# One-hot tiles of the column keys, written by VectorE token by token instead of number by number

## The chip, the core and the metric

The kernel runs on one core of one Trainium2 chip. The metric is the device time of one execution in microseconds (us), the median of three runs. The core's engines are called as in the profile: PE is TensorE's matmuls, PEld its weight loads, DVE VectorE, ACT ScalarE, POOL GpSimd, SP SyncE, whose queue issues the plain DMAs.

## What is computed

One inference step of a two-layer decoder for 512 prompt tokens and 8 sample tokens. Layer 0 is a gated MLP, layer 1 differential attention, and a PEER block stands behind each. PEER picks, for every token and each of 8 heads, 16 of 16,384 experts by two small top-16 searches (a row key and a column key, 128 each), and adds the chosen experts' outputs. The part of the reference that matters here:

```python
s = jnp.einsum('thcd,hcnd->thcn', q, keys)
sv, si = lax.top_k(s, PEER_TOPK)
...
cidx = si[:, :, 0, :, None] * N_KEYS + si[:, :, 1, None, :]
top_s, pos = lax.top_k(cand, PEER_TOPK)
eidx = jnp.take_along_axis(cidx, pos, axis=-1)
g = jax.nn.softmax(top_s, axis=-1)
act = jax.nn.gelu(jnp.einsum('thkd,td->thk', u_tab[eidx], h))
return jnp.einsum('thk,thkd->td', (g * act).astype(h.dtype), v_tab[eidx])
```

## The kernel before

PEER is done in two ways at once. For two of the four prompt tiles of 128 tokens in each layer (256 tokens), `dense_peer` goes through all 16,384 experts with matmuls. For the other two, `peer_tile` gathers the chosen rows by indirect DMA, 256 rows of u and of v (128x1024 each) per tile, and DVE multiplies them (lines 715 and 722). These 512 gathers a layer are spread over the dense work: a table of anchors ties each of them to an instruction of the dense part, and the scheduler that writes each engine's order of instructions keeps them behind it. Every engine then runs its instructions in the fixed order of the built program.

The dense part goes through the experts in four quarters `q` of 32 row keys each (`QI` = 32, with 128 column keys to a row key).

- `acts(q)` (lines 478 to 500): for each row key, the 128 experts' activations for 256 tokens, with u from DMA. In quarter 0 these are fp32 matmuls (line 494). In the others u is split into a high and a low part by ACT (`wh`, line 209) and DVE (`wl`, line 211), and three series of 8 matmuls follow (lines 488, 489, 491). The gelu goes into `W`.
- `gates(q)` (lines 502 to 537): the gate of each token and expert, as a product of two one-hot matrices. For each token there is a stationary operand `ohj` (128 picked experts x 128 column keys, f16: 1 where the expert has that column key) and a moving operand `gi` (128 picked experts x 32 row keys, the gate where the row key fits). Two matmuls (line 533; the gate's high and low half) give a token's 128x32 gates, each with its own weight load of `ohj`. `W` is multiplied by the result (line 536).
- `y` (lines 565 to 576): the gated activations times v, summed over all experts in PSUM.

A tile of `ohj` holds 8 tokens, 1,024 numbers per partition. In each group of four tiles (32 tokens) the first `J_DVE[layer][q]` are written by DVE and the others by ACT. With `J_DVE = [[2, 1, 1, 1], [2, 2, 2, 2]]` and 8 groups to a quarter, DVE writes 40 tiles in layer 0 and 64 in layer 1, which is 104 of 256.

- DVE (line 520): one instruction compares the column keys of 8 tokens with `iotaJ` (128x8 numbers, each column key eight times). The tile is stored number by number: key 0 for all 8 tokens, key 1 for all 8 tokens, and so on. The 128 weights of one token then stand 8 elements (16 bytes) apart.
- ACT (lines 526 and 529): eight instructions |iota - key|, one for each token, and one relu(1 - x) over the tile. The tile is stored token by token: the 128 weights of one token are adjacent.

The weight load of line 533 reads `oh[:, :, k]`, strided from the first kind of tile and packed from the second.

The gates of quarter 0 run beside `acts(1)` before the first `y`. The gates of the later quarters run beside `y` of the quarter before them:

```python
        for _ in gates(0):
            for _ in range(2):
                next(na, None)
```

Of the kernel before, what the change touches and what calls it, by code (L numbers as in the profile page):

```python
# [11 lines left out]
HF = mybir.dt.float16  # L12
# [23 lines left out]
def body(ctx: ExitStack, tc: tile.TileContext, a):  # L36
# [26 lines left out]
    rows = [128, 128, 128, 128, NB]  # L63
    iota128 = const("iota128", [128, 128])

    iotaJ = per.tile([128, 128, 8], HF, name="iotaJ")
    V.tensor_copy(iotaJ, iota128[:, :, None].to_broadcast([128, 128, 8]))
    msk64 = const("msk64", [64, H, 16])
    r64 = const("r64", [64, NB])
    r64f = per.tile([64, NB], FR, name="r64f")  # L70
# [328 lines left out]
    def topk_pick(p, nh, state, layer, gp, out):  # L399
        sv, si, ts, pos = [v[:p] for v in state]  # L400
        n = nh * 16
        tmp = wk.tile([128, 1024], F32, name="tmp", tag="tmp", bufs=1)[:p]
        t1, t2 = [tmp[:, k * 128:k * 128 + n].bitcast(U32) for k in range(2)]
        af, st = [tmp[:, k * 128:k * 128 + n] for k in (2, 3)]
        ab = tmp[:, 512:640].bitcast(HF).rearrange("p (c n) -> p c n", c=2)[:, :, :n]
        sib = tmp[:, 640:768].bitcast(HF)[:, :2 * n].rearrange("p (c k h) -> p c k h", c=2, k=16)
        ij = tmp[:, 768:1024].rearrange("p (c n) -> p c n", c=2)[:, :, :n]
        V.tensor_copy(sib.rearrange("p c k h -> p h c k"), si)

        g = ts if gp is None else gp.tile([128, nh, 16], F32, name="gate", tag="gate", bufs=2)[:p]  # L410
        sm = small(p, nh, "gs")
        V.tensor_copy(sm[:, :, None], ts[:, :, 0:1])
        V.tensor_tensor(g, ts, sm[:, :, None].to_broadcast([p, nh, 16]), op=OP.subtract)
        SC.activation(g, g, AF.Exp)
        yield

        pf = pos.rearrange("p h k -> p (h k)")
        V.tensor_scalar(t1, pf, 4, None, op0=OP.logical_shift_right)
        V.tensor_scalar(t2, pf, 2, None, op0=OP.logical_shift_right)
        V.scalar_tensor_tensor(af, t2, -12.0, t1, op0=OP.add, op1=OP.max)  # L420
        V.scalar_tensor_tensor(af, pf, -72.0, af, op0=OP.add, op1=OP.max)
        yield
        V.tensor_scalar(st, af, 4.0, 48.0, op0=OP.mult, op1=OP.add)
        V.scalar_tensor_tensor(st, af, 16.0, st, op0=OP.mult, op1=OP.min)
        V.scalar_tensor_tensor(st, af, 72.0, st, op0=OP.add, op1=OP.min)

        kh = [ab[:, c].rearrange("p (k h) -> p h k", k=16) for c in range(2)]
        V.tensor_copy(kh[0], af.rearrange("p (h k) -> p h k", h=nh))
        V.tensor_tensor(kh[1], pos, st.rearrange("p (h k) -> p h k", h=nh), op=OP.subtract)
        yield  # L430
        V.tensor_reduce(sm, g, axis=AX.X, op=OP.add)
        V.reciprocal(sm, sm)
        V.tensor_tensor(g, g, sm[:, :, None].to_broadcast([p, nh, 16]), op=OP.mult)
        yield
        for c in range(2):
            oh = wk.tile([128, 16, n], HF, name="oh", tag="junk", bufs=1)[:p]
            m, w = n // 8, 8
            V.tensor_tensor(oh.rearrange("p x (m w) -> p x m w", m=m),
                            ab[:, c, None, :].rearrange("p x (m w) -> p x m w", m=m).to_broadcast([p, 16, m, w]),
                            iotaJ[:p, :16, None, :w].to_broadcast([p, 16, m, w]), op=OP.is_equal)  # L440
            yield
            o4 = oh.rearrange("p x (k h) -> p x k h", k=16)
            V.tensor_tensor(o4, o4, sib[:, c, :, None, :].to_broadcast([p, 16, 16, nh]), op=OP.mult)
            yield
            for x in (8, 4, 2):
                V.tensor_tensor(oh[:, :x], oh[:, :x], oh[:, x:2 * x], op=OP.add)
            V.tensor_tensor(ij[:, c, :].rearrange("p (h k) -> p k h", h=nh),
                            oh[:, 0].rearrange("p (k h) -> p k h", k=16),
                            oh[:, 1].rearrange("p (k h) -> p k h", k=16), op=OP.add)
            yield  # L450
        V.tensor_scalar(ij[:, 1], ij[:, 1], float(layer * NE), None, op0=OP.add)
        out += [ij, g, tmp]
# [16 lines left out]
    def dense_peer(layer, dpa, open_rest, open_odd, smp):  # L469
# [32 lines left out]
        def gates(q):  # L502
# [4 lines left out]
            for t0 in range(0, 256, 32):  # L507

                gi = dpb.tile([128, 2, 16, QI, 2], HF, name="gi", tag="gi", bufs=2)
                sv = [z[:, t0:t0 + 32].rearrange("p (m w) -> p m w", w=2)[:, :, None, :].to_broadcast([128, 16, QI, 2])  # L510
                      for z in (sq, selb[:, 2], selb[:, 3])]
                V.tensor_tensor(gi[:, 1], sv[0], iotaP[:, None, :QI, :].to_broadcast([128, 16, QI, 2]), op=OP.is_equal)
                for k in range(2):
                    V.tensor_tensor(gi[:, k], gi[:, 1], sv[1 + k], op=OP.mult)  # L514
                for t1 in range(t0, t0 + 32, 16):
                    ps = pt.tile([128, QI, 16], F32, name="ps_g", tag="tr")
                    for t2 in range(t1, t1 + 16, 8):
                        oh = dpb.tile([128, 128, 8], HF, name="ohj", tag="ohj", bufs=4)
                        if (t2 // 8) % 4 < J_DVE[layer][q]:
                            V.tensor_tensor(oh, selb[:, 1, None, t2:t2 + 8].to_broadcast([128, 128, 8]), iotaJ,  # L520
                                            op=OP.is_equal)
                        else:

                            oh = oh.rearrange("p j k -> p (j k)").rearrange("p (k j) -> p j k", k=8)
                            for k in range(8):
                                SC.activation(oh[:, :, k], iota128, AF.Abs, scale=-1.0,  # L526
                                              bias=selJ[:, t2 + k:t2 + k + 1])
                            oh2 = oh.rearrange("p j k -> p k j")
                            SC.activation(oh2, oh2, AF.Relu, bias=1.0, scale=-1.0)
                        for k in range(8):  # L530
                            t = t2 + k
                            for c in range(2):
                                PE.matmul(ps[:, :, t - t1], oh[:, :, k], gi[:, c, (t - t0) // 2, :, t % 2], start=c == 0,  # L533
                                          stop=c == 1)
                    wv = W[q][:, :, t1:t1 + 16]
                    tick(V.tensor_tensor(wv, ps, wv, op=OP.mult), [[4, 7, 3, 3], [3, 1, 1, 1]][layer][q])
                    yield
# [3 lines left out]
        drain()  # L541
        dpb, py = open_rest()

        iotaP = dpb.tile([128, 128, 2], HF, name="iotaP")
        V.tensor_copy(iotaP, iotaJ[:, :, :2])
        y = [[py.tile([128, 512], F32, name=f"y{t}{hf}", tag=f"y{t}{hf}") for hf in range(2)] for t in range(2)]
        odd = open_odd()
        na = acts(1)
# [657 lines left out]
```

## Time and profile before

| | us |
|---|---|
| median of 3 runs (lowest, highest) | 3229.25 (3229.22, 3231.66) |
| the profiled execution | 3223.32 |
| its span in the trace | 3221.6 |
| PE busy | 2987.1 (93%) |
| DVE busy | 2435.9 (76%) |
| ACT busy | 1306.8 (41%) |
| POOL busy | 1339.0 (42%) |

The span runs from the first to the last instruction of the program; the profiled execution takes 1.7 us more than it. Busy times are of whole engines over the whole span. Matmuls overlap, so their busy time is a union of modelled durations; in a timeline, a row with xN is N instructions that follow each other, with the time from the first's start to the last's end.

### The profile page before, as it was taken

To read this page: it belongs to the slowest core of one execution; us is meant where nothing else is said; L and a number is where in the kernel's file an instruction comes from. 1 tells how busy PE (TensorE), PEld (TensorE's weight loads), DVE (VectorE), ACT (ScalarE), POOL (GpSimd) and SP (SyncE) were. 2 spreads that over 40 slices of the span, in tenths; PEclk is the share of its full clock that TensorE was granted. 3 is DMA by queue.
4 is the path that set the end of the run, shared out by engine and by line. 5 is a ranking of instruction groups with operands and counts; after the bars stand their busy time and mean duration, and the time that the engine had idled before them with its cause. 6 is when DMAs were issued, how large, how long until landed. Compare 5 with 4: busy or idle time off the path is not lost.

```text
span 3221.6 us, 49841 instructions
## 1 busy us (share of the span) xinstructions
PE 2987.1 (93%) x18048; PEld 2237.7 (69%) x18048; DVE 2435.9 (76%) x5119; ACT 1306.8 (41%) x2940; POOL 1339.0 (42%) x1061
## 2 busy tenths in 40 slices
PE   7998979999999999999789988788799999999999
PEld 7898646788558758767687643455689658758767
DVE  1389779769877687789646788879979886686785
ACT  2344021246564573655343333321246443363444
POOL 0035672014554354455511665534234454344340
PEclk9999989999999999999999988799899999999999
DMA  7678987458999899999976989867778999889895
GB/s 246 227 278 303 332 330 247 157 194 305 376 375 366 304 353 357 338 355 368 353 245 203 368 317 320 279 245 269 273 263 305 351 356 360 326 315 357 321 318 171
DMA packets 271561, 976.53 MB, mean 303 GB/s; under 512 B 30938, under 2 KB 31770, under 8 KB 271306
## 3 DMA queue, kind: packets, MB, share of 16 engines
q0 software_dynamic: 152064, 553.72, 47.4%
q1 hardware_dynamic: 119250, 419.62, 36.5%
q8 instruction: 142, 2.33, 0.3%
q14 instruction: 105, 0.86, 0.1%
HBM read 966.76 MB, written 6.46 MB: 302 GB/s over the span
## 4 chain that ended last, share of the span: by engine, by line
PE 66%; DVE 11%; DMA 11%; issue 6%; ACT 4%; POOL 3%; SPq 0%; DVEq 0%; POOLq 0%; ACTq 0%
PE y L576 18%; PE ps_d L231 8%; PE ps_a L494 6%; PE ps_a L488 6%; PE ps_a L489 6%; PE ps_a L491 5%; PE ps_g L533 5%; DMA gath<-peer_v,ix 4%; DMA gath<-peer_u,ix 3%; POOL gath L706 3%; DVE x L722 2%; ACT ohj L526 2%; DVE gath L715 2%; DVE si L369 1%; DMA page<-cache_v 1%
## 5 line engine op out<-in xcount | busy, mean ns | idle before, releaser
L706 POOL DMA_INDIRECT gath<-peer_u,ix x512 | 652.3, 1274 | 921.9 <-DVE gath L715 316.7
L706 POOL DMA_INDIRECT gath<-peer_v,ix x512 | 649.1, 1268 | 700.2 <-DVE x L722 350.9
L722 DVE SCALAR_TENSOR_TENSOR x<-gath,act,x 128x1024 f32<-128x1024 f32 x512 | 655.4, 1280 | 66.0 <-DMA gath<-peer_v,ix 59.5
L576 PE MATMUL y<-vb,W 128*128 128x512 f32 x1536 | 697.8, 600 | 2.1 <-DMA vb<-peer_v 2.1
L715 DVE SCALAR_TENSOR_TENSOR gath<-gath,h_g 128x1024 f32<-128x1024 f32 x512 | 614.8, 1218 | 97.4 <-DMA gath<-peer_u,ix 96.2
L576 PEld LDWEIGHTS y<-vb,W 128*128 128x128 f32 x1536 | 280.7, 191 | 297.0 <-issue 294.3
L231 PE MATMUL ps_d<-hT,wt 128*128 128x128 f32 (+3 forms) x2048 | 432.6, 370 | 28.8 <-DMA wt<-peer_wq 6.7
L526 ACT ACTIVATE ohj<-iota,selJ 128x128 f16<-128x128 f32 x1216 | 367.1, 387 | 216.3 <-PE ps_g L533 215.8
L488 PE MATMUL ps_a<-hPh,wh 128*128 128x256 f32 x1536 | 400.8, 298 | 14.7 <-ACT wh L209 14.7
L231 PEld LDWEIGHTS ps_d<-hT,wt 128*128 128x128 f32 x2048 | 306.3, 200 | 141.5 <-issue 21.0
L489 PE MATMUL ps_a<-hPl,wh 128*128 128x256 f32 x1536 | 384.3, 287 | 0.0
L211 DVE TENSOR_TENSOR wl<-ub,wh 128x1024 fp32r<-128x1024 f32 x192 | 234.6, 1223 | 196.7 <-ACT wh L209 179.2
L488 PEld LDWEIGHTS ps_a<-hPh,wh 128*128 128x128 f32 x1536 | 298.4, 194 | 29.5 <-ACT wh L209 17.2
L209 ACT ACTIVATE wh<-ub 128x1024 fp32r<-128x1024 f32 x192 | 202.0, 1054 | 274.6 <-PE ps_a L489 246.0
L489 PEld LDWEIGHTS ps_a<-hPl,wh 128*128 128x128 f32 x1536 | 298.4, 194 | 10.8 <-issue 10.8
L494 PE MATMUL ps_a<-hT,ub 128*128 128x256 f32 x1024 | 229.6, 386 | 25.1 <-ACT W L499 25.1
L494 PEld LDWEIGHTS ps_a<-hT,ub 128*128 128x128 f32 x1024 | 197.0, 194 | 54.4 <-ACT W L499 25.9
L533 PEld LDWEIGHTS <-ohj 128*128 128x128 f16 x4096 | 190.8, 127 | 62.5 <-issue 48.4
L499 ACT ACTIVATE W<-ps_a 128x256 f32<-128x256 f32 x256 | 95.6, 379 | 341.7 <-PE ps_a L491 180.8
L491 PE MATMUL ps_a<-hPh,wl 128*128 128x256 f32 x1536 | 223.1, 288 | 1.9 <-DVE wl L211 1.9
L533 PE MATMUL ps_g<-gi,ohj 128*128 128x32 f16 x4096 | 197.0, 206 | 12.4 <-DVE gi L514 9.4
L491 PEld LDWEIGHTS ps_a<-hPh,wl 128*128 128x128 f32 x1536 | 200.2, 193 | 9.0 <-issue 5.8
(299 smaller groups left out, 3810.4 us busy)
## 6 DMA issues: line engine op xcount, KB each, us to landing
ub<-peer_ut SPq DMA_DIRECT2D x256, 512.0 KB, 5.8
vb<-peer_v SPq DMA_DIRECT2D x256, 512.0 KB, 6.5
wt<-w_in SPq DMA_DIRECT2D x64, 512.0 KB, 4.5
wt<-peer_wq SPq DMA_DIRECT2D x64, 512.0 KB, 4.7
wt<-w_out SPq DMA_DIRECT2D x32, 512.0 KB, 5.4
gath<-peer_u,ix POOLq DMA_INDIRECT x512, 6.7
gath<-peer_v,ix POOLq DMA_INDIRECT x512, 6.9
wt<-w_k SPq DMA_DIRECT2D x16, 512.0 KB, 5.6
```

Source lines behind the costliest of these rows:

```text
L211: tick(V.tensor_tensor(wl, w, wh.bitcast(F32), op=OP.subtract), k)
L231: z = PE.matmul(ps[:, :n], wt[:, c, :], rhs[:, c0 + c, :n], start=c0 + c == 0, stop=c0 + c == nk - 1)
L488: PE.matmul(ps, uh[:, c, :], hP[0][:, c, :], start=c == 0, stop=False)
L489: PE.matmul(ps, uh[:, c, :], hP[1][:, c, :], start=False, stop=False)
L491: PE.matmul(ps, ul[:, c, :], hP[0][:, c, :], start=False, stop=c == 7)
L494: z = PE.matmul(ps, u[:, c, :], hT[:, c, :256], start=c == 0, stop=c == 7)
L526: SC.activation(oh[:, :, k], iota128, AF.Abs, scale=-1.0, bias=selJ[:, t2 + k:t2 + k + 1])
L533: PE.matmul(ps[:, :, t - t1], oh[:, :, k], gi[:, c, (t - t0) // 2, :, t % 2], start=c == 0, stop=c == 1)
L576: PE.matmul(y[t][hf], w[:, ts], v[:, hs], start=i == 0, stop=i == 127)
L706: GP.indirect_dma_start(out=t, out_offset=None, in_=table, in_offset=bass.IndirectOffsetOnAxis(ap=ix[:, k:k + 1], axis=0))
L715: z = V.scalar_tensor_tensor(u, u, 1.0, h, op0=OP.mult, op1=OP.mult, accum_out=act[:, k:k + 1])
L722: z = V.scalar_tensor_tensor(x[t], v, act[:, k:k + 1], x[t], op0=OP.mult, op1=OP.add)
```

## The change

DVE's tiles are stored token by token as well. For that, the column keys are written twice each into a new tile `selJ2` (256 tokens x 2), and the comparison of line 520 goes over 8 tokens x 64 pairs of keys x 2, so that its innermost run is two adjacent numbers. `iotaJ` (1,024 numbers) is replaced by `iotaH` (128), for that comparison, and `iota8` (16x8), for the top-16 searches; `iotaP` shrinks from 256 numbers to 64. All weight loads of the gates now read a packed `oh[:, k, :]`. ACT's instructions and the numbers that are computed stay the same.

```diff
-    iotaJ = per.tile([128, 128, 8], HF, name="iotaJ")
-    V.tensor_copy(iotaJ, iota128[:, :, None].to_broadcast([128, 128, 8]))
+    iotaH = per.tile([128, 128], HF, name="iotaH")
+    V.tensor_copy(iotaH, iota128)
+    iota8 = per.tile([128, 16, 8], HF, name="iota8")
+    V.tensor_copy(iota8, iota128[:, :16, None].to_broadcast([128, 16, 8]))
...
-                        oh = dpb.tile([128, 128, 8], HF, name="ohj", tag="ohj", bufs=4)
+
+                        oh = dpb.tile([128, 8, 128], HF, name="ohj", tag="ohj", bufs=4)
                         if (t2 // 8) % 4 < J_DVE[layer][q]:
-                            V.tensor_tensor(oh, selb[:, 1, None, t2:t2 + 8].to_broadcast([128, 128, 8]), iotaJ,
-                                            op=OP.is_equal)
+                            V.tensor_tensor(oh.rearrange("p k (m w) -> p k m w", w=2),
+                                            selJ2[:, t2:t2 + 8, None, :].to_broadcast([128, 8, 64, 2]),
+                                            iotaH[:, None, :].to_broadcast([128, 8, 128])
+                                            .rearrange("p k (m w) -> p k m w", w=2), op=OP.is_equal)
                         else:
-
-                            oh = oh.rearrange("p j k -> p (j k)").rearrange("p (k j) -> p j k", k=8)
                             for k in range(8):
-                                SC.activation(oh[:, :, k], iota128, AF.Abs, scale=-1.0,
+                                SC.activation(oh[:, k, :], iota128, AF.Abs, scale=-1.0,
                                               bias=selJ[:, t2 + k:t2 + k + 1])
...
-                                PE.matmul(ps[:, :, t - t1], oh[:, :, k], gi[:, c, (t - t0) // 2, :, t % 2], start=c == 0,
+                                PE.matmul(ps[:, :, t - t1], oh[:, k, :], gi[:, c, (t - t0) // 2, :, t % 2], start=c == 0,
...
-        iotaP = dpb.tile([128, 128, 2], HF, name="iotaP")
-        V.tensor_copy(iotaP, iotaJ[:, :, :2])
+        iotaP = dpb.tile([128, QI, 2], HF, name="iotaP")
+        V.tensor_copy(iotaP, iotaH[:, :QI, None].to_broadcast([128, QI, 2]))
+        selJ2 = dpb.tile([128, 256, 2], HF, name="selJ2")
+        V.tensor_copy(selJ2, dd["sel"][1][:, 1, :, None].to_broadcast([128, 256, 2]))
```

The scheduler writes the orders anew, so some instructions move. On DVE, where the gates of layer 0's quarter 0 begin, the order before is:

```order
L545 COPY iotaP<-iotaJ 128x256
L506 TENSOR_SCALAR selq<-selb 128x256
L520 TENSOR_TENSOR ohj<-selb,iotaJ 128x1024 x2
L512 TENSOR_TENSOR gi<-selq,iotaP 128x1024 x2
L514 TENSOR_TENSOR gi<-gi,selb 128x1024 x4
```

At the same place on DVE, the order of the changed kernel (whose line numbers are 2 to 4 higher) is:

```order
L547 COPY iotaP<-iotaH 128x64
L549 COPY selJ_4455<-selb 128x512
L508 TENSOR_SCALAR selq<-selb 128x256
L523 TENSOR_TENSOR ohj<-selJ_4455,iotaH 128x1024 x2
L514 TENSOR_TENSOR gi<-selq,iotaP 128x1024 x2
L516 TENSOR_TENSOR gi<-gi,selb 128x1024 x4
```

One copy (`selJ2`, printed as `selJ_4455`) has come in ahead of the first two `ohj` and of the `gi` behind them; the rest stands as it stood.

A little later in the same quarter, where the `wl` of `acts(1)` alternate with the gathered tiles (`x_70<-gath` is line 722, `gath,act<-gath` line 715), DVE's order before is:

```order
L512 TENSOR_TENSOR gi<-selq,iotaP 128x1024
L722 SCALAR_TENSOR_TENSOR x_70<-gath,act,x_70 128x1024
L514 TENSOR_TENSOR gi<-gi,selb 128x1024
L722 SCALAR_TENSOR_TENSOR x_70<-gath,act,x_70 128x1024
L514 TENSOR_TENSOR gi<-gi,selb 128x1024
L722 SCALAR_TENSOR_TENSOR x_70<-gath,act,x_70 128x1024
L211 TENSOR_TENSOR wl<-ub,wh 128x1024
L520 TENSOR_TENSOR ohj<-selb,iotaJ 128x1024
L536 TENSOR_TENSOR W<-ps_g,W 128x32x16
```

At that place DVE's order in the changed kernel is:

```order
L514 TENSOR_TENSOR gi<-selq,iotaP 128x1024
L726 SCALAR_TENSOR_TENSOR x_70<-gath,act,x_70 128x1024
L516 TENSOR_TENSOR gi<-gi,selb 128x1024
L726 SCALAR_TENSOR_TENSOR x_70<-gath,act,x_70 128x1024
L516 TENSOR_TENSOR gi<-gi,selb 128x1024
L213 TENSOR_TENSOR wl<-ub,wh 128x1024
L726 SCALAR_TENSOR_TENSOR x_70<-gath,act,x_70 128x1024
L523 TENSOR_TENSOR ohj<-selJ_4455,iotaH 128x1024
L538 TENSOR_TENSOR W<-ps_g,W 128x32x16
```

A `wl` has changed places with one gathered tile. Moves of this kind, mostly by a few places, occur all through the dense part of both layers, on every engine, and here and there in layer 1's attention, where the rest of the gathers is placed. Each engine still has the same work between the start and the end of each part, up to one or two gathered tiles.

## Rows read from the trace of the kernel before

**Rows 1.** The page: busy time by engine, and the chain that ended last.

```profile
PE 2987.1 (93%) x18048; PEld 2237.7 (69%) x18048; DVE 2435.9 (76%) x5119; ACT 1306.8 (41%) x2940; POOL 1339.0 (42%) x1061
...
PE 66%; DVE 11%; DMA 11%; issue 6%; ACT 4%; POOL 3%; SPq 0%; DVEq 0%; POOLq 0%; ACTq 0%
```

**Rows 2.** Tile view of `ohj`: ns min/median/max, first and last start, form.

```profile
L533 PEld LDWEIGHTS <-ohj x4096: 95/98/208, 687.4 to 3116.5; 128*128 128x128 f16 x196
...
L526 ACT ACTIVATE ohj<-iota,selJ x1216: 384/387/406, 683.6 to 3107.3; 128x128 f16<-128x128 f32 x174
L529 ACT ACTIVATE ohj<-ohj x152: 1038/1042/1058, 688.2 to 3108.5; 128x1024 f16<-128x1024 f16 x152
L520 DVE TENSOR_TENSOR ohj<-selb,iotaJ x104: 670/682/705, 684.3 to 3099.4; 128x1024 f16<-128x1024 f16 x104
```

**Rows 3.** Timeline of weight loads, layer 0's first gates, then one of layer 1's.

```profile
691.88 1.95 PEld L533 LDWEIGHTS <-ohj 128*128 128x128 f16 x31
...
696.62 0.99 PEld L533 LDWEIGHTS <-ohj 128*128 128x128 f16 x32
...
2501.75 2.04 PEld L533 LDWEIGHTS <-ohj 128*128 128x128 f16 x32
```

**Rows 4.** Timelines of DVE and ACT: who wrote layer 0's first four `ohj`.

```profile
684.30 1.29 DVE L520 TENSOR_TENSOR ohj<-selb,iotaJ 128x1024 f16<-128x1024 f16 x2
...
688.25 1.99 ACT L529 ACTIVATE ohj<-ohj 128x1024 f16<-128x1024 f16 x2
```

**Rows 5.** Four stretches of dense work: length, busy us, granted clock, DMA share, GB/s.

```profile
684.00:830.00 146.00, 131.26 (x1293) 123.64 (x1294) 131.21 (x172) 103.51 (x234) 72.07 (x51) 0.96 0.83 286
830.00:1420.00 590.00, 586.64 (x3970) 399.98 (x3969) 445.61 (x585) 319.91 (x762) 286.32 (x237) 1.00 0.95 353
2380.00:2500.00 120.00, 109.19 (x1110) 105.07 (x1111) 106.17 (x137) 85.36 (x196) 50.48 (x35) 0.96 0.79 280
2500.00:3200.00 700.00, 697.88 (x4478) 491.36 (x4478) 524.05 (x682) 294.94 (x641) 296.62 (x244) 1.00 0.89 326
```

(Busy times in the order PE, PEld, DVE, ACT, POOL, each with its count of instructions.)

**Rows 6.** The same stretches, `ohj` alone: busy us and counts of PE, PEld, DVE, ACT.

```profile
684.00:830.00 146.00, 26.74 (x512) 24.46 (x512) 11.55 (x17) 64.41 (x170) 0.96 0.83 286
830.00:1420.00 590.00, 65.88 (x1536) 64.95 (x1536) 15.78 (x23) 231.52 (x621) 1.00 0.95 353
2380.00:2500.00 120.00, 23.62 (x448) 21.52 (x448) 10.83 (x16) 52.43 (x141) 0.96 0.79 280
2500.00:3200.00 700.00, 80.76 (x1600) 79.87 (x1600) 32.81 (x48) 165.13 (x437) 1.00 0.89 326
```

**Rows 7.** Waits of PE in 684:830, then in 2380:2500: us, times, longest.

```profile
PE ps_a L488 <- ACT wh L209: 9.3, 5, 3.4
PE ps_g L533 <- DVE gi L514: 3.7, 1, 3.7
...
PE ps_g L533 <- DVE gi L514: 5.7, 1, 5.7
PE ps_a L488 <- ACT wh L209: 5.3, 3, 2.6
```

**Rows 8.** Timeline of PE behind one such wait, its first and last slow matmuls.

```profile
735.32 0.58 PE L488 MATMUL ps_a<-hPh,wh 128*128 128x256 f32 x1 [1.40 <-ACT wh L209]
...
738.25 0.28 PE L489 MATMUL ps_a<-hPl,wh 128*128 128x256 f32 x1
738.36 0.28 PE L488 MATMUL ps_a<-hPh,wh 128*128 128x256 f32 x1
```

**Rows 9.** Prices on DVE, by line: ns min/median/max, or (L715) busy us, mean ns.

```profile
L512 DVE TENSOR_TENSOR gi<-selq,iotaP x64: 670/680/685, 685.5 to 3094.0; 128x1024 f16<-128x1024 f16 x64
...
L545 DVE COPY iotaP<-iotaJ x2: 261/262/263, 684.0 to 2382.0; 128x256 f16<-128x256 f16 x2
...
L715 DVE SCALAR_TENSOR_TENSOR gath<-gath,h_g 128x1024 f32<-128x1024 f32 x512 | 614.8, 1218 | 97.4 <-DMA gath<-peer_u,ix 96.2
```

**Rows 10.** 50 us of layer 0's last gates, columns as in Rows 5.

```profile
1350.00:1400.00 50.00, 49.34 (x378) 27.13 (x378) 44.55 (x60) 47.34 (x129) 27.42 (x23) 1.00 0.93 339
```

More of the change, by code (lines that the diff above doesn't have):

```diff
@@ L439, in topk_pick @@
                             ab[:, c, None, :].rearrange("p x (m w) -> p x m w", m=m).to_broadcast([p, 16, m, w]),
-                            iotaJ[:p, :16, None, :w].to_broadcast([p, 16, m, w]), op=OP.is_equal)
+                            iota8[:p, :, None, :w].to_broadcast([p, 16, m, w]), op=OP.is_equal)
             yield
@@ L511, in gates @@
                       for z in (sq, selb[:, 2], selb[:, 3])]
-                V.tensor_tensor(gi[:, 1], sv[0], iotaP[:, None, :QI, :].to_broadcast([128, 16, QI, 2]), op=OP.is_equal)
+                V.tensor_tensor(gi[:, 1], sv[0], iotaP[:, None, :, :].to_broadcast([128, 16, QI, 2]), op=OP.is_equal)
                 for k in range(2):
@@ L517, in gates @@
                     for t2 in range(t1, t1 + 16, 8):
-                        oh = dpb.tile([128, 128, 8], HF, name="ohj", tag="ohj", bufs=4)
+                        oh = dpb.tile([128, 8, 128], HF, name="ohj", tag="ohj", bufs=4)
                         if (t2 // 8) % 4 < J_DVE[layer][q]:
-                            V.tensor_tensor(oh, selb[:, 1, None, t2:t2 + 8].to_broadcast([128, 128, 8]), iotaJ,
-                                            op=OP.is_equal)
+                            V.tensor_tensor(oh.rearrange("p k (m w) -> p k m w", w=2),
+                                            selJ2[:, t2:t2 + 8, None, :].to_broadcast([128, 8, 64, 2]),
+                                            iotaH[:, None, :].to_broadcast([128, 8, 128])
+                                            .rearrange("p k (m w) -> p k m w", w=2), op=OP.is_equal)
                         else:
-                            oh = oh.rearrange("p j k -> p (j k)").rearrange("p (k j) -> p j k", k=8)
                             for k in range(8):
-                                SC.activation(oh[:, :, k], iota128, AF.Abs, scale=-1.0,
+                                SC.activation(oh[:, k, :], iota128, AF.Abs, scale=-1.0,
                                               bias=selJ[:, t2 + k:t2 + k + 1])
-                            oh2 = oh.rearrange("p j k -> p k j")
-                            SC.activation(oh2, oh2, AF.Relu, bias=1.0, scale=-1.0)
+                            SC.activation(oh, oh, AF.Relu, bias=1.0, scale=-1.0)
                         for k in range(8):
```

## The prediction, made before the changed kernel was run

> **What bounds the kernel now.** I read the whole span first. PE is busy for 93% of it, no other engine for more than 76%, and the chain that ended last is PE for 66% [rows 1]. Such an average says nothing of a stage, so I cut out the four stretches in which `ohj` is used [rows 5]: layer 0's quarter 0 (684 to 830), its later gates (830 to 1420), and the same two of layer 1 (2380 to 2500, 2500 to 3200). In the two long ones PE is busy for 586.64 of 590 us and 697.88 of 700, at a granted clock of 1.00, with DVE at 446 and 524 us. There whatever shortens PE's stream shortens the stretch. In the two short ones PE is idle for 14.7 of 146 us and 10.8 of 120, and DVE is busy for 90% and 88%. Two engines are near their limit there, and PE does wait, for the split of u (`wh`) and for `gi` [rows 7].
>
> Next I looked at `ohj` itself. The weight load of line 533 has one form, yet lasts between 95 and 208 ns [rows 2], so two kinds lie behind the group. Its timeline shows them [rows 3]. At 691.88, 31 loads follow each other in 1.95 us; at 696.62, 32 take 0.99 us. Who wrote which tile is seen from the writers [rows 4]: DVE's first two `ohj` are finished at 685.59, ACT's first two at 690.24, and the loop takes DVE's tiles first. So the slow loads are of DVE's tiles, whose weights lie 8 elements apart, and the fast ones of ACT's packed tiles. Layer 1 repeats it: 32 loads take 2.04 us. Both kinds belong to the same matmul, with 32 columns and the same `gi`. The loads lie back to back, so at this place PE's pace is the pace of its weight loads.
>
> **The change, part by part.**
>
> The weight loads. Two tiles are 32 loads, strided 2.04 us, packed 0.99 us [rows 3]: 1.05 us apart. Some 0.05 to 0.07 of it is the last load's own length, which the next matmul may cover, so I take 1.00 us for two tiles and 0.50 for one. DVE writes 104 tiles [rows 2], and the four stretches hold 17, 23, 16 and 48 of them [rows 6]. At 0.50 us that is 8.5, 11.5, 8.0 and 24.0 us of PE's time, 52 in all. What becomes of it differs:
>
> - 2500 to 3200: PE waits for next to nothing, ACT is at 42% and DVE at 75% [rows 5]. I take 23 of 24.
> - 830 to 1420: PE is full as well, but in layer 0 ACT writes three tiles of four, and in the last gates it is busy for 47.34 of 50 us [rows 10]. A faster PE soon waits for ACT's tile there. DMA, at a share of 0.95, has less room than in layer 1 too. Bounds 5 and 11.5, taken 8: this quarter's 8 tiles would give 4 us, most of which I write off.
> - 684 to 830: the split chain ACT `wh`, DVE `wl`, PE and DVE's 90% hold the pace together with PE. Bounds 0 and 8.5; half, 4.
> - 2380 to 2500: the same with less gathering, as PE waits for `wh` 5.3 us instead of 9.3 [rows 7]. Bounds 0 and 8; 5.5.
>
> The comparison on DVE. The new instruction has 1,024 f16 elements with an innermost run of two, one input repeated over the middle dimension and the other over the outer one. The trace has that very shape: line 512 compares `selq` with `iotaP` in the same way, in 680 ns [rows 9], against 682 ns for line 520 [rows 2]. So its cost stays. If it lost the fast form, the nearest row is an fp32 instruction of 1,024 elements, 1218 ns [rows 9]: 104 x 0.54 = 56 us more on DVE, of which the 33 tiles of the short stretches, 18 us, would lie on DVE near its limit, and the rest in DVE's idle quarter of the long ones. I take zero.
>
> The copies. `selJ2` (512 elements) is new, ahead of the first `gi`, for which PE waits 3.7 and 5.7 us [rows 7], so it is on the path once per layer. It costs between the 0.26 us of `iotaP`'s 256 elements [rows 9] and the 0.68 of a 1,024-element instruction [rows 2]; I take 0.4, less 0.1 for the shorter `iotaP`: 0.3 a layer, 0.6 in all. The smaller iota tiles at the start of the kernel replace one short instruction by two and lie ahead of a stage that needs neither; nothing.
>
> The order. `wl` and gathered tiles change places by one or two in DVE's queue. A `wl` that now stands behind a gathered tile reaches PE 1.2 us later, one that stands ahead of it 1.2 us earlier. In the long stretches DVE's idle quarter covers that; in the short ones PE feels it, in either direction. I take zero, with 6 us to either side.
>
> Nothing else is added: DMA bytes, gathers, ACT's work and the matmuls are the same. The gathers are tied to the dense work in DVE's fixed order, so they move forward with it. The shorter time asks for some 3% more DMA rate than 353 and 326 GB/s [rows 5].
>
> Sum: 23 + 8 + 4 + 5.5 - 0.6 = 39.9, say 40 us off the profiled execution's 3223.3, which leaves 3183. The median of the runs shown lies 5.9 us above that execution, so I expect a median of 3229.25 - 40 = 3189 us.
>
> [...]
>
> **The rivals.**
>
> *All of it arrives.* The short stretches and layer 0's gates follow PE too, and the new order happens to help. For it: PE is busy for 90% and 91% even in the short ones. Against: the waits there. 52 - 0.6 gives 3178 us; with the order's luck 3171.
>
> *Hidden in part.* Only where PE waits for nothing and no other engine is near its limit does it count: layer 1's 23 us, less the copies. ACT, DVE and the gathers hold layer 0 at its pace. For it: ACT's 47.34 of 50, and DVE's 90% of the first stretch. Against: in 830 to 1420 as a whole PE is idle for 3.4 us of 590. 3229 - 22 = 3207 us.
>
> *The layout is not the cause.* The two kinds of tiles differ in the writing engine too, and if the slow loads came from that, nothing changes but the copies: 3230 us. Against: the slow pace lasts through all 31 loads, long after DVE has finished writing. [...]
>
> *Slower: the new order makes PE wait for `wl`.* DVE works in order, and a `wl` behind a gathered tile comes 1.2 us later. In quarter 0 of each layer acts(1) has 32 of them, 64 in all. It decides from the point where the delays eat up the gain: 40 / 1.2 = 33 of the 64 would have to become later with PE waiting for each. If all 64 did, the loss would be 64 x 1.2 - 40 = 37 us: 3266. A wait can also cost clock: behind a wait at 735.32 the 14 matmuls up to 738.25 took 2.93 us where 13 steps of 0.11 (738.25 to 738.36) make 1.4, so 1.5 us were lost [rows 8]. Against: at the place shown, a `wl` moved ahead of a gathered tile; the moves go both ways.
>
> **How the numbers follow.** Gains of 34 to 46 us, my sum with its small errors, get 0.55; more than that (to 58) 0.18; hidden in part (10 to 34) 0.18; layout not the cause or all hidden, within 0.2%, 0.05; slower 0.04. A measurement of this kernel tells from no change about 0.2%, which is 6.5 us. The predicted time is that of the likeliest case, 3189 us. The range 3170 to 3213 us takes in gains of 16 to 59 us: the first two cases and most of the third, about 0.85. Faster 0.91, same 0.05, slower 0.04.
>
> **What the changed profile would show.** The weight loads of `ohj` have one length, near 98 ns, and 32 of them take 0.99 us whoever wrote the tile; if some still take 2.04, the layout is not the cause. The comparison stays at 0.68 us; 1.2 would mean that the innermost pair costs the fast form. PE's busy time falls by some 50 us, while its idle time grows by about 11: in the two quarters 0, and before matmuls that wait for ACT's `ohj` in layer 0's last gates. If it grows there by more than 25 us, the second rival is right. If PE's waits for `wl` and `wh` grow beyond what the packed loads give, the order is to blame. The prediction would be wrong altogether if PE's stream in the long stretches were paced by something that the busy time covers up, such as the transfers of v: then the loads would get faster and the stretches stay as long.

## The result, and the profile after

The changed kernel takes 3196.8 us (median of 4 runs, 3192.31 to 3199.41), the kernel before 3230.45 (4 runs, 3229.22 to 3242.16). The ratio, estimated from all of these runs, is 0.9886, with a 95% interval of 0.9861 to 0.9912: 37 us less, between 28 and 45. (The two medians alone lie 33.7 us apart.) The profiled execution took 3197.43 us, with a span of 3195.7. The forecast was 3189 us, in a range of 3170 to 3213.

The page's busy time answers to [rows 1]: PE's busy time is 37.0 us shorter, DVE's and ACT's are within 4 us of what they were, and POOL's is 11 us longer. (The chain that ended last could be followed back over only 37% of this span, so it is not set beside the one of before.)

```profile
PE 2950.1 (92%) x18048; PEld 2188.9 (68%) x18048; DVE 2432.4 (76%) x5122; ACT 1307.6 (41%) x2940; POOL 1350.4 (42%) x1061
```

The tile view of `ohj` after (ns min/median/max, first and last start, form), for [rows 2]:

```profile
L535 PEld LDWEIGHTS <-ohj x4096: 95/98/291, 686.9 to 3090.5; 128*128 128x128 f16 x196
...
L529 ACT ACTIVATE ohj<-iota,selJ x1216: 384/387/404, 682.8 to 3080.5; 128x128 f16<-128x128 f32 x174
L531 ACT ACTIVATE ohj<-ohj x152: 1037/1043/1059, 687.5 to 3081.0; 128x1024 f16<-128x1024 f16 x152
L523 DVE TENSOR_TENSOR ohj<-selJ,iotaH x104: 669/682/722, 683.8 to 3073.2; 128x1024 f16<-128x1024 f16 x104
```

DVE's comparison costs 682 ns, as before, although its innermost run is now two numbers. And the two kinds of loads are gone, as the timeline of weight loads in layer 0's first gates shows. DVE's first tiles (31 loads in view) come at 691.38, ACT's at 695.25, and both have the pace that only ACT's had in [rows 3]:

```profile
691.38 0.96 PEld L535 LDWEIGHTS <-ohj 128*128 128x128 f16 x31
...
695.25 0.99 PEld L535 LDWEIGHTS <-ohj 128*128 128x128 f16 x32
```

The four stretches of dense work, cut again at the stages' new edges (columns as in [rows 5]):

```profile
683.00:820.00 137.00, 123.73 (x1307) 114.84 (x1306) 130.27 (x172) 104.77 (x236) 69.94 (x48) 0.99 0.85 298
820.00:1410.00 590.00, 581.75 (x3983) 391.25 (x3983) 447.81 (x592) 319.68 (x762) 294.88 (x240) 0.99 0.95 357
2377.00:2490.00 113.00, 102.55 (x1108) 97.79 (x1108) 105.69 (x138) 84.03 (x194) 56.00 (x35) 0.95 0.81 292
2490.00:3175.00 685.00, 675.68 (x4483) 468.18 (x4483) 522.83 (x682) 298.03 (x642) 297.04 (x244) 1.00 0.90 334
```

The same with `ohj` alone (busy us and counts of PE, PEld, DVE, ACT), for [rows 6]:

```profile
683.00:820.00 137.00, 18.77 (x512) 16.16 (x512) 11.54 (x17) 65.28 (x171) 0.99 0.85 298
820.00:1410.00 590.00, 53.49 (x1536) 51.65 (x1536) 15.82 (x23) 230.81 (x621) 0.99 0.95 357
2377.00:2490.00 113.00, 16.71 (x448) 14.25 (x448) 10.88 (x16) 52.12 (x140) 0.95 0.81 292
2490.00:3175.00 685.00, 57.89 (x1600) 55.32 (x1600) 32.78 (x48) 166.07 (x437) 1.00 0.90 334
```

PE's busy time for the 4,096 gate matmuls is 146.9 us where it was 197.0 (26.74 + 65.88 + 23.62 + 80.76). That is 50.1 us less, 0.48 us for each of DVE's 104 tiles. The whole of PE lost only 37.0, because the rest of its work was 13 us longer in this execution, 10 of them in layer 1's attention; in the second pair of traces (experiment 7) PE lost 46.5 (2988.8 to 2942.3). PE's idle time in the four stretches, length less busy time, is 41.3 us where it was 31.0; the forecast had some 11 more. The main waits of PE in the first, second and fourth stretch show what it waits for (us in total, times, longest), for [rows 7]:

```profile
PE ps_a L490 <- ACT wh L211: 5.4, 5, 1.7
PE ps_g L535 <- DVE gi L516: 3.9, 1, 3.9
PE ps_a L493 <- DVE wl L213: 3.0, 2, 2.4
...
PE ps_hb L735 <- DVE W L538: 5.2, 3, 4.3
PE ps_g L535 <- ACT ohj L531: 0.7, 1, 0.7
...
PE ps_y L749 <- DMA gaths<-peer_v,ixs: 4.4, 1, 4.4
```

Two more lines of the trace of before belong beside them, the first from 684 to 830, the second from 830 to 1420:

```profile
PE ps_a L491 <- DVE wl L211: 1.9, 3, 1.1
...
PE ps_g L533 <- ACT ohj L529: 0.7, 2, 0.4
```

In the first stretch the waits for the split (`wh`, `wl`) sum to 8.4 us, where they had 11.2. In the second, ACT's `ohj` costs 0.7 us, as it did before, though the forecast had written off 3.5 to ACT and DMA there. Two waits are new. One is for DVE's product `W` (`ps_hb`), 4.35 us of it at 838.59. It comes with the new order: it is 0.4 us in the kernel before and in experiment 1, 2.9 in experiment 2 and 5.5 in the second trace of the changed kernel. The other is 4.4 us in layer 1's long stretch for the gathered samples, of which the second trace of the changed kernel has 1.2:

```profile
PE ps_y L749 <- DMA gaths<-peer_v,ixs: 1.2, 1, 1.2
```

### The profile page after: what moved, and what is told of

The parts are those of the page before. It is cut to its first block, busy times and chain, and to the rows that moved or that the text cites. A ratio compares the mean times of both kernels' runs of the same rounds, so it can differ in the third digit from the quotient of the medians.

```text
span 3195.7 us, 49835 instructions
## 1 busy us (share of the span) xinstructions
PE 2950.1 (92%) x18048; PEld 2188.9 (68%) x18048; DVE 2432.4 (76%) x5122; ACT 1307.6 (41%) x2940; POOL 1350.4 (42%) x1061
## 5 line engine op out<-in xcount | busy, mean ns | idle before, releaser
L529 ACT ACTIVATE ohj<-iota,selJ 128x128 f16<-128x128 f32 x1216 | 367.1, 388 | 189.2 <-PE ps_g L535 188.8
L490 PE MATMUL ps_a<-hPh,wh 128*128 128x256 f32 x1536 | 397.6, 296 | 11.5 <-ACT wh L211 11.4
L535 PEld LDWEIGHTS <-ohj 128*128 128x128 f16 x4096 | 137.4, 99 | 67.5 <-issue 49.5
L535 PE MATMUL ps_g<-gi,ohj 128*128 128x32 f16 x4096 | 146.9, 194 | 13.9 <-DVE gi L516 10.2
```

Source lines behind the costliest of these rows:

```text
L490: PE.matmul(ps, uh[:, c, :], hP[0][:, c, :], start=c == 0, stop=False)
L529: SC.activation(oh[:, k, :], iota128, AF.Abs, scale=-1.0, bias=selJ[:, t2 + k:t2 + k + 1])
L535: PE.matmul(ps[:, :, t - t1], oh[:, k, :], gi[:, c, (t - t0) // 2, :, t % 2], start=c == 0, stop=c == 1)
```

## The experiments

Each is timed against runs of the kernel before on the same chip, whose medians were 3236.02, 3235.4 and 3234.48 in the three groups (17, 9 and 17 runs). The groups ran on different chips, so it is the ratios that can be compared. A difference in us is the ratio's, taken of that median.

**1. The layout alone, in the old order.** The kernel before with one line, by which PE reads DVE's tiles packed. Its instructions and their order on every engine are those of before.

```diff
                             V.tensor_tensor(oh, selb[:, 1, None, t2:t2 + 8].to_broadcast([128, 128, 8]), iotaJ,
                                             op=OP.is_equal)
+                            oh = oh.rearrange("p j k -> p (j k)").rearrange("p (k j) -> p j k", k=8)
```

> The kernel before, in its order instruction for instruction and with its own comparison on DVE; only PE reads DVE's tiles packed instead of strided. The tiles are still stored number by number, so the gates of DVE's tokens are wrong numbers; the work is the same. Theory (the gain is the weight loads alone): 3190 to 3203 us, as the changed kernel. Rival (part of the gain or a loss is due to the new order of instructions): if the new order helps, 3205 to 3220; if it costs, 3180 to 3190.

Measured: 3197.0 us (3192.54 to 3205.32), ratio 0.9893 (0.9875 to 0.9911), 35 us less. The tile view has one kind of load:

```profile
L534 PEld LDWEIGHTS <-ohj x4096: 94/98/291, 683.2 to 3085.4; 128*128 128x128 f16 x196
```

**2. The rest of the change without the layout.** The changed kernel, with its order and its instructions, where only PE reads DVE's tiles 8 elements apart.

```diff
                                             .rearrange("p k (m w) -> p k m w", w=2), op=OP.is_equal)
+                            oh = oh.rearrange("p k j -> p (k j)").rearrange("p (j k) -> p k j", k=8)
```

> The changed kernel, in its order instruction for instruction, with its new comparison and copies on DVE; only PE reads DVE's tiles strided, 8 elements apart, as before. The tiles are stored token by token, so the gates of DVE's tokens are wrong numbers; the work is the same. Theory: 3224 to 3237 us, as the kernel before. Rival (the order gives part of the gain): 3205 to 3222; if the order costs: 3238 to 3250.

Measured: 3238.32 us (3232.49 to 3246.34), ratio 1.0011 (0.9998 to 1.0023). So the new order, the copies and the other comparison together cost between nothing and 7 us beside the slow loads; beside the fast ones they cost nothing that can be seen (0.9886 with them, 0.9893 without, in experiment 1). The layout of what PE reads is the whole gain, to within these few us.

**3. Everything strided.** The kernel before, where ACT writes number by number too, and every load reads with a step of 8 elements.

```diff
-                            oh = oh.rearrange("p j k -> p (j k)").rearrange("p (k j) -> p j k", k=8)
                             for k in range(8):
...
-                            oh2 = oh.rearrange("p j k -> p k j")
-                            SC.activation(oh2, oh2, AF.Relu, bias=1.0, scale=-1.0)
+                            SC.activation(oh, oh, AF.Relu, bias=1.0, scale=-1.0)
```

> The kernel before, in its order, with ACT's 152 tiles stored number by number too, so that all 4,096 weight loads are strided. Theory (PE's stream sets the pace of the dense part): 152 x 0.5 = 76 us more on PE, of which three quarters to all arrive: 3285 to 3306 us. Rival (layer 0 is held by ACT, DVE or DMA and follows PE in part only): only layer 1's 64 tiles and some of layer 0's count, 3255 to 3275. If the writing engine and not the layout made the loads slow: 3230.

Measured: 3489.95 us (3477.3 to 3504.72), ratio 1.0803 (1.0778 to 1.0828), far above what either theory gave. The experiment had changed two things. The tile view shows that ACT's write of 128 elements at a step of 16 bytes takes 1077 ns instead of 387. The busy time of all 1,216 (the page's first number behind the bar) doubles, from 367.1 us in the kernel before to 734.4; it grows less than the single durations, since one overlaps the next:

```profile
L525 ACT ACTIVATE ohj<-iota,selJ x1216: 846/1077/1173, 682.4 to 3362.3; 128x128 f16<-128x128 f32 x174
...
L526 ACT ACTIVATE ohj<-iota,selJ 128x128 f16<-128x128 f32 x1216 | 367.1, 387 | 216.3 <-PE ps_g L533 215.8
...
L525 ACT ACTIVATE ohj<-iota,selJ 128x128 f16<-128x128 f32 x1216 | 734.4, 1069 | 155.6 <-PE ps_g L531 155.3
```

and the largest waits of PE over the whole span are for ACT, first for its `ohj` tiles:

```profile
PE ps_g L531 <- ACT ohj L527: 69.2, 32, 5.5
PE ps_a L488 <- ACT wh L209: 63.0, 15, 7.7
```

So it says nothing clean of the loads, and the next one separates them.

**4. All loads strided, all writes as before.** ACT writes packed; PE alone reads its tiles with the step too.

```diff
                             SC.activation(oh2, oh2, AF.Relu, bias=1.0, scale=-1.0)
+                            oh = oh2.rearrange("p k j -> p (k j)").rearrange("p (j k) -> p j k", k=8)
```

> The kernel before, in its order instruction for instruction, DVE and ACT writing their tiles as before; only PE reads ACT's 152 packed tiles strided too, 8 elements apart, so the gates of ACT's tokens are wrong numbers and the work is the same. It replaces the run in which ACT wrote its tiles strided, where ACT's own instructions became 2.8 times as long. The 1,664 loads of the change gave 47 us of PE's stream, 28 ns each. Theory (PE's stream is the pace, and four fifths of a change in it arrive): 2,432 x 28 ns = 68 us more on PE, 50 to 62 us more in all, 1.5% to 1.9% above the kernel before. Rival (the dense part is held elsewhere too): 15 to 40 us more.

Measured: 3307.61 us (3295.59 to 3313.85), ratio 1.0231 (1.0209 to 1.0253), 75 us more (68 to 82), above the 50 to 62 that were expected. The loads of ACT's tiles are now as slow as DVE's were, so the writing engine has nothing to do with it:

```profile
L534 PEld LDWEIGHTS <-ohj x4096: 141/173/207, 686.3 to 3188.6; 128*128 128x128 f16 x196
```

PE's busy time for the gates (`ps_g`; first PE, then DVE; layer 0, then layer 1) is 273.0 us:

```profile
680.00:1650.00 970.00, 136.56 (x2048) 44.14 (x64) 0.98 0.90 330
2370.00:3480.00 1110.00, 136.41 (x2048) 44.17 (x64) 0.99 0.69 252
```

With 0, 104 and 256 tiles read strided it is 146.9, 197.0 and 273.0 us: 0.48 us a tile for the first 104 and 0.50 for the next 152. The time follows: of the 76.0 us of the second step nearly all arrive, 75 (68 to 82) by the runs and 67 to 69 by the traces (layer 0's first gate to layer 1's attention, and layer 1's first gate to its last `y`, against the two traces of the kernel before). One load more costs 31 ns here, where 28 had been taken.

**5. More of the tiles to DVE.** The changed kernel, with ACT relieved in layer 0: if ACT holds its later gates, this frees them.

```diff
-        J_DVE = [[2, 1, 1, 1], [2, 2, 2, 2]]
+        J_DVE = [[2, 2, 2, 2], [2, 2, 2, 2]]
```

> The changed kernel with two of four tiles written by DVE in all quarters of layer 0, instead of one of four in quarters 1 to 3: 24 tiles go from ACT (4.1 us each) to DVE (0.68 us). If ACT holds layer 0's later gates, as I took it to when I wrote off some 3 us there: 3190 to 3194 us. If the gathers or DVE hold them, or nothing but PE does: 3196 to 3200.

Measured: 3201.24 us (3198.58 to 3212.82), ratio 0.9899 (0.9883 to 0.9915). No gain is seen. DVE has 128 tiles instead of 104 and ACT 1,024 comparisons instead of 1,216:

```profile
L529 ACT ACTIVATE ohj<-iota,selJ x1024: 384/387/404, 686.5 to 3097.8; 128x128 f16<-128x128 f32 x171
...
L523 DVE TENSOR_TENSOR ohj<-selJ,iotaH x128: 668/684/723, 687.4 to 3090.8; 128x1024 f16<-128x1024 f16 x128
```

Between 820 and 1410 ACT is busy for 246.9 us instead of 319.7, and PE for 578.0 instead of 581.8 of the 590. That agrees with ACT not holding the stretch. By itself the run does not settle 3 us, since its interval is 5 us to either side, and PE's waits for DVE's `W` went from 5.2 to 7.3 us. What settles it is the 0.7 us for which PE waits for ACT's `ohj` there in the changed kernel.

**6. The packed tile without the pairs.** DVE compares as before, with the tokens innermost, but writes the packed tile, so that neighbours in its order lie 256 bytes apart.

```diff
+                            oh = oh.rearrange("p j k -> p (j k)").rearrange("p (k j) -> p j k", k=8)
                             V.tensor_tensor(oh, selb[:, 1, None, t2:t2 + 8].to_broadcast([128, 128, 8]), iotaJ,
                                             op=OP.is_equal)
```

> The packed tile without the pairs: DVE compares as before (8 tokens innermost, the same inputs), but writes its result token by token, so that neighbours in its output lie 128 elements apart. All weight loads are packed; the result is right. If the output's step takes the fast form away, 0.54 us more for each of 104 tiles on DVE (1.22 instead of 0.68), 56 us, of which the 33 tiles of the two quarters 0 lie where DVE is near its limit: some 10 to 18 us of the gain of 35 are lost, 3211 to 3220 on the scale where the kernel before is at 3236. If scattered 2-byte writes cost DVE as much as they cost ACT (2.8 times, 1.9 us): 127 us more on DVE, 3225 to 3260. If the step costs nothing: 3197 to 3203, and the pairs were not needed.

Measured: 3552.63 us (3544.26 to 3564.7), ratio 1.0991 (1.0964 to 1.1019). The loads are all fast, but the comparison takes 4714 ns, 6.9 times as long, and far above the 1.9 us that were expected at most; the fp32 row that the forecast had taken as the upper bound of a slow comparison is at 1218 [rows 9].

```profile
L534 PEld LDWEIGHTS <-ohj x4096: 95/98/291, 695.0 to 3444.3; 128*128 128x128 f16 x196
...
L521 DVE TENSOR_TENSOR ohj<-selb,iotaJ x104: 4670/4714/4944, 683.9 to 3420.4; 128x1024 f16<-128x1024 f16 x104
```

The packed tile is worth 50 us of PE; the pairs save 104 x 4.03 = 419 us of DVE that this other way of packing costs.

**7. Both kernels once more**, unchanged, for a second pair of traces.

> The kernel before once more, with a profile. Its attention of layer 1 (first to last score transpose) took 430.3 us in the first profile and 445.1 us in the changed kernel's, which hides 15 us of what the dense parts gained. If that is the scatter of one execution: some value between 428 and 450 here, unrelated to the kernel. If it is the change: 429 to 432 here and 444 to 446 in the repeat of the changed kernel.

> The changed kernel once more, with a profile. Dense part of layer 0 (first gate matmul to last y matmul) 819.6 us and of layer 1 808.1 us in its first profile, 833.3 and 830.8 before: both should repeat within 3 us. Attention of layer 1: if its length is the scatter of one execution, anything between 428 and 450; if the change lengthens it, 444 to 446.

Measured: 3232.94 us before and 3195.07 after, with spans of 3231.3 and 3193.4. The dense parts were to repeat within 3 us, and three of the four did: layer 0's with 833.7 us before (833.3 in the first profile) and 820.4 after (819.6), layer 1's with 807.7 after (808.1), but 836.0 before (830.8). Layer 1's attention took 436.1 us before and 448.3 after; the next section comes back to it.

**8 and 9. How far apart may the elements lie?** All loads again, now 4 elements (8 bytes) apart, then 2 (4 bytes). Both writers are as before. The edit for 4:

```diff
+                            oh = oh.rearrange("p j k -> p (j k)").rearrange("p (h j w) -> p j h w", j=128, w=4)
                         else:
...
+                            oh = oh2.rearrange("p k j -> p (k j)").rearrange("p (h j w) -> p j h w", j=128, w=4)
                         for k in range(8):
...
-                                PE.matmul(ps[:, :, t - t1], oh[:, :, k], gi[:, c, (t - t0) // 2, :, t % 2], start=c == 0,
+                                PE.matmul(ps[:, :, t - t1], oh[:, :, k // 4, k % 4], gi[:, c, (t - t0) // 2, :, t % 2], start=c == 0,
```

> The kernel before, with DVE and ACT writing as there, but all 4,096 weight loads of ohj read their 128 columns 4 elements (8 bytes) apart instead of 8 (16 bytes). The gates' numbers change for all tokens; the instructions and their order are those before. Theory one, the distance decides: two neighbours that are read one after the other lie in the same 16 bytes, and the loads keep the pace of the packed ones, 98 ns median and 0.99 us for 32; the time is then that of the kernel before with packed loads, 3197 us, within 10. [...] Theory two, any step other than one element costs the same: 173 ns median, 2.04 us for 32, and 3307 us as with 16 bytes. A pace between the two, near 1.5 us for 32, would give some 3250.

> The same with a step of 2 elements (4 bytes) for all 4,096 loads; the gates' numbers change for all tokens. Theory one, the distance decides: 98 ns, 3197 us. Theory two, any step costs the same: 173 ns, 3307 us. If the cost grows with the step: clearly less than what the 4-element step costs, some 1.2 us for 32 and 3220.

Measured for 4: 3204.48 us (3190.43 to 3214.47), ratio 0.9901 (0.9871 to 0.9931); for 2: 3195.49 us (3177.73 to 3197.87), ratio 0.9876 (0.9826 to 0.9926). The tile view of the first, and PE's busy time for its gates (as in experiment 4):

```profile
L535 PEld LDWEIGHTS <-ohj x4096: 111/118/181, 687.9 to 3106.7; 128*128 128x128 f16 x196
...
680.00:1650.00 970.00, 81.03 (x2048) 43.56 (x64) 0.98 0.92 343
2370.00:3480.00 1110.00, 81.25 (x2048) 43.84 (x64) 0.99 0.67 244
```

The tile view of the second:

```profile
L535 PEld LDWEIGHTS <-ohj x4096: 95/98/181, 684.8 to 3070.6; 128*128 128x128 f16 x196
```

A step of 2 costs nothing. A step of 4 costs 20 ns a load, and 15.4 us of gate time over all 256 tiles (162.3 against 146.9), against 126.1 for a step of 8. The runs do not resolve these 15.4 us: the intervals for 4 and for 2 overlap. So "strided" is the wrong word for what is slow: it is the distance. Theory one holds, but for the 15.4 us.

**10. The same for ACT's writes.** The kernel before, with ACT's comparison written 4 elements apart.

```diff
+                            ow = oh.rearrange("p j k -> p k j").rearrange("p k j -> p (k j)").rearrange("p (h j w) -> p j h w", j=128, w=4)
                             for k in range(8):
-                                SC.activation(oh[:, :, k], iota128, AF.Abs, scale=-1.0,
+                                SC.activation(ow[:, :, k // 4, k % 4], iota128, AF.Abs, scale=-1.0,
```

> The kernel before, where ACT's 1,216 comparisons write their 128 elements 4 elements (8 bytes) apart, and its 152 second passes and PE's loads go over the tile as before, so that the gates' numbers change for the tokens that ACT compares. Written packed one takes 387 ns, written 8 elements (16 bytes) apart 1077 ns. Theory one, the distance decides: 387 ns again, and the time of the kernel before, 3235 us within 10. Theory two, any step costs: 1077 ns, 840 us more of ACT's time, and a kernel near 3420 us, since all strided gave 3490, of which some 72 are the strided loads. A cost in proportion would lie near 700 ns.

Measured: 3238.75 us (3225.91 to 3246.53), ratio 1.0005 (0.998 to 1.003). One write lasts 550 ns, between packed (387) and 16 bytes apart (1077). But the next one starts long before it ends. Sixteen in a row take 5.01 us, against 4.81 packed and 9.73 at 16 bytes, as timelines of this run, of the kernel before and of experiment 3 show, and the busy time of all 1,216 is 387.9 us (the first line's first number behind the bar) against 367.1 and 734.4:

```profile
L527 ACT ACTIVATE ohj<-iota,selJ x1216: 536/550/613, 686.2 to 3125.4; 128x128 f16<-128x128 f32 x174
...
L527 ACT ACTIVATE ohj<-iota,selJ 128x128 f16<-128x128 f32 x1216 | 387.9, 554 | 209.9 <-PE ps_g L534 209.4
...
701.19 5.01 ACT L527 ACTIVATE ohj<-iota,selJ 128x128 f16<-128x128 f32 x16 [0.16 <-PE ps_g L534]
...
697.36 4.81 ACT L526 ACTIVATE ohj<-iota,selJ 128x128 f16<-128x128 f32 x16 [0.16 <-PE ps_g L533]
...
696.76 9.73 ACT L525 ACTIVATE ohj<-iota,selJ 128x128 f16<-128x128 f32 x16 [0.62 <-PE ps_g L531]
```

So ACT has only some 21 us more to do, and by its pace theory one holds for the writes too, to within 6%. A single duration is not the cost where instructions overlap. That the time did not move (6 us less to 10 more) therefore says little of the room that ACT has in the gates.

## Why the prediction was right, step by step

**The loads.** "0.50 for one" tile was read from two rows of one timeline. It is 0.48 by PE's busy time, and 0.45 by a second count: in a pair of kernels with the same order, the k-th matmul of one trace is the k-th of the other, so the start of each gate matmul can be taken from the start of the next one, where that is a gate matmul too, and summed. That gives 46.5 us for 104 tiles in the old order and 47.3 in the new. The forecast's 52 was 2 to 6 us too high. One load of the first two tiles stands apart, at 687.4 [rows 2], from the 31 in a row [rows 3]; that such a load costs PE no more when it is strided is the author's estimate for the rest, and was not shown.

**What arrives.** The same count gives the length of each stretch, cut at the same matmuls, without and with the slow loads. In the table, the stream is what the gate matmuls themselves got shorter, and what arrives is what the stretch got shorter, both in us:

| stretch | tiles | forecast: stream, arrives | stream, old order / new | arrives, old order / new |
|---|---|---|---|---|
| 684 to 830 | 17 | 8.5, 4 | 7.7 / 8.0 | 4.9 / 9.0 |
| 830 to 1420 | 23 | 11.5, 8 | 10.5 / 10.6 | 9.9 / 10.3 |
| 2380 to 2500 | 16 | 8.0, 5.5 | 7.0 / 7.0 | 6.2 / 5.2 |
| from 2500 on | 48 | 24, 23 | 21.3 / 21.7 | 18.2 / 19.3 |
| sum | 104 | 52, 40.5 | 46.5 / 47.3 | 39.2 / 43.8 |

The old order is the kernel before against experiment 1, the new one experiment 2 against the changed kernel, cut at the changed kernel's edges (683, 820, 2377, 2490), which hold the same numbers of gate matmuls. The sum is right and its terms are not: by this count the stream was taken 5 us too long and what is lost of it 4 to 8 us too large. That these two errors nearly cancel is luck.

- In 830 to 1420 nearly all arrives. "A faster PE soon waits for ACT's tile there" was the wrong step. ACT's 47 of 50 busy us [rows 10] are spent on tiles that PE does not yet ask for: the wait is 0.7 us after the change (1.6 in experiment 1) and was 0.7 before it, and experiment 5, which takes work from ACT, shows no gain. A busy share was read as a hold, where only a wait behind that engine would have shown one.
- From 2500 on 2 to 3 us of the stream do not arrive in these pairs, where the forecast had 1 ("23 of 24", since "PE waits for next to nothing"). PE, now earlier, does wait for the gathered samples: 4.4 us, 1.2 in the second trace of the changed kernel, 3.5 in experiment 1 and 0.9 in experiment 2, and not at all in the two traces of before. But against the second trace of before, experiment 1 gains 22.0 us here, all of its stream. So 2 to 3 us lie within the scatter of single traces, and their cause is not shown.
- In 684 to 830 half was taken, and 4.9 to 9.0 came, at most 0.5 us over the upper bound; in 2380 to 2500, 5.5 was taken and 5.2 to 6.2 came, within the bounds.

**The comparison** was priced at no change, by line 512, which has the same shape. It costs 682 ns as before. Its upper bound for a slow form, 1218 ns, was far too low for a scattered write (experiment 6), but that form is not the one in the change. That an f16 comparison could take 1218 ns was an estimate from the fp32 row [rows 9]; the runs have 682 to 685 and 4714.

**The copies.** The timeline of DVE has 0.42 us for the new copy and 0.18 for `iotaP`, against 0.26 [rows 9]; the forecast's 0.3 a layer is 0.34.

```profile
683.22 0.18 DVE L547 COPY iotaP<-iotaH 128x64 f16<-128x64 f16 x1
683.32 0.42 DVE L549 COPY selJ<-selb 128x512 f16<-128x512 f16 x1
```

**The order**, "zero, with 6 us to either side": experiment 2 measures 3.6 us more, between 0.6 less and 7.4 more. In the profiles, attention of layer 1 looks like its place. The first and last transposes of its weights start at these times, in the changed kernel:

```profile
L918 PE MATMUL ps_at<-ident,p_sm x80: 272/417/476, 1596.9 to 2042.0; 128*128 128x128 f32 x80
```

and in the kernel before:

```profile
L914 PE MATMUL ps_at<-ident,p_sm x80: 272/330/476, 1614.9 to 2045.2; 128*128 128x128 f32 x80
```

That is 445.1 us against 430.3. But the second trace of before has 436.1 and experiment 1, in the old order, 440.5; and from there to layer 1's first gate it is 340.3 us after and 344.7 and 345.0 in those two. Both parts together take 785.4 us after the change (787.4 in its second trace, 781.9 in experiment 2) and 770.6, 780.8 and 785.5 in the old order. The four runs with other loads or writes in the old order spread further, from 774.5 to 792.1. So the first trace of before is the shortest of all, the traces of the new order lie within the scatter of the old one, and the 15 us between the first two profiles say nothing of the change. What the order does by itself stays open within the 7 us.

**From 40 us to the median.** From layer 0's first gate to layer 1's attention, the two pairs of traces save 17.4 and 15.8 us, and from layer 1's first gate to its last `y` 22.7 and 28.3: 40.1 and 44.1, where the forecast had 40. The span of the first pair fell only by 25.9, since before's own execution was quick in attention; that of the second by 37.9. The 28.3 holds the 836.0 us of before's second trace, which was 5 us longer there than the first. The forecast moved the median by the sum alone: 3230.45 - 39.9 would be 3190.6, and 3196.8 was measured. The 6 us between lie within the interval of the ratio.

**The rivals.** *The layout is not the cause* fell with experiments 1, 2 and 4. Nor is every step slow: loads at steps of 1 and 2 elements take the same (98 ns), at 4 nearly the same (118), and at 8 not (173, experiment 4). ACT's writes show it by their pace: 367.1 us busy packed, 387.9 at a step of 4 and 734.4 at 8. That two neighbours in the same 16 bytes make the difference, as the expectation for the step of 4 has it, and not the distance as such, is the author's estimate and not shown, since the two change together here. *All of it arrives* (3178) came nearest for the share, 39.2 to 43.8 of 46.5 to 47.3 us, but its 52 us were never there, and no run of the changed kernel took less than 3192. *Hidden in part* (3207) is refuted by layer 0, which gave 15 to 19 us in the table; the time alone would not have done it, as 33.7 us by the medians lies at the edge between this case and the forecast. *Slower by `wl`* would have shown in experiment 2, which has that order without the gain, at 1.0011. The clock that it names is in the trace of before: behind the wait of 1.40 us at 735.32, a granted clock of 0.50 from 735.3 to 738.1, and 1.00 from 738.2 to 745.

## What to carry to other kernels

Where one line's weight loads have a wide spread of durations, look in a timeline for two kinds, and then at how far apart in memory the elements lie that one load reads: 4 bytes cost nothing for a load here, 8 bytes a fifth of its 98 ns, and 16 bytes make 32 loads take twice as long (2.04 us against 0.99). Let 16-bit weights lie in the order in which they are read, and let the engines write in that same order (DVE's comparison took 4714 ns instead of 682 when written 256 bytes apart, and ACT's comparisons were busy for 734.4 us instead of 367.1 when written 16 bytes apart). Where an input that is repeated breaks it, store that input in pairs, as here, at 682 ns; single numbers in that order were not run. Where a stretch is bound by one engine, don't write off gain to another engine because it is busy; look for a wait behind it (ACT was busy for 47 of 50 us in layer 0's last gates, and PE waited 0.7 us for its tiles in all of 830 to 1420). Where instructions of one engine overlap, price them by the busy time of the group or by a row of them, not by the duration of one (16 of ACT's, of 550 ns each, took 5.01 us).

## What the runs showed of the hardware that was not expected

- A weight load of 128 f16 columns takes 98 ns at a step of 1 or 2 elements, 118 at 4 and 173 at 8.
- ACT's write of 128 f16 elements lasts 387 ns packed, 550 at a step of 4 elements and 1077 at 8, but 16 in a row take 4.81, 5.01 and 9.73 us: at a step of 4 one gets longer and the pace hardly changes.
- DVE's comparison of 1,024 f16 elements takes 682 ns written packed, also with its inputs read in pairs, and 4714 when its output neighbours lie 256 bytes apart.
